# Attention on one core: a root chain for each tile of queries and keys, without rows in DRAM, and half of the wide high parts on GpSimd

## The chip, the cores and the metric

The kernel runs on one NeuronCore of one Trainium2 chip. The metric is the device time of one execution in microseconds. Engines are named as in the profile: PE is TensorE (PEld its weight loads), DVE VectorE, ACT ScalarE, POOL GpSimd, SP SyncE, whose queue here issues nearly all DMAs.

## The reference

A trunk of two layers over 1024 positions and 1024 features: a recurrent block with an MLP, then chunked band attention with an MLP. The stage that the change touches is the attention of the second layer:

```python
h = rmsnorm(x, kv_norm)
kv = (h @ w_kv).reshape(bsz, s, 2, N_HEADS, HEAD_DIM)
k = rmsnorm(kv[:, :, 0], k_norm)
v = kv[:, :, 1]
...
q = (rmsnorm(h, b_norm[j]) @ b_w_q[j]).reshape(bsz, s, N_HEADS, HEAD_DIM)
q = rmsnorm(q, b_q_norm[j])
...
sc = jnp.einsum('bhqd,bhkd->bhqk', qb, kb).astype(jnp.float32) * scale + bias
p = jax.nn.softmax(sc, axis=-1).astype(vb.dtype)
return jnp.einsum('bhqk,bhkd->bhqd', p, vb)
```

There are 16 heads of 64 features. Each query or key vector of 64 features is divided by the root of its mean square (rmsnorm with EPS 1e-6). A query sees its own chunk of 64 positions and the eight before it.

## The kernel before

Everything is held with features on partitions: a tile t (0 to 7) is 128 features, which is two heads, by 1024 positions, worked on in two halves h of 512. Products of 32-bit data are made of a high and a low part, three matmuls each (`mm`, L376 to L378).

In the attention stage the work of a tile is of two sorts.

*Projections* (`Proj`). For keys, queries and values in turn, 16 steps each (two halves by eight tiles of x, three matmuls a step) fill a bank `pj`. `normed` then normalizes a half of keys or queries: it scales it (q, L1726), squares it on ScalarE (L1729, L1732), and splits the squares in sh and sl (sl on GpSimd, L1735). Two matmuls (L1744, L1745) with a constant `band` sum the squares of each head. `band` is ones in 2 x 64 rows by 16 columns and is read at an offset, so that the four halves j of a tile (two of keys, two of queries) add their sums to different rows of one bank `nm`: 16 equal rows for each half and head. There is one `nm` bank, which is taken at j = 0. After j = 3 `roots` makes the inverse roots of all eight rows at once: Ln, Exp and Square on ScalarE (L1794, L1796, L1799), two operations on VectorE (L1801, which frees the bank, and L1805). One row of each 16 is written to DRAM (`rd`), and four DMAs read it back as `rb`, each spreading two rows of 512 numbers over 2 x 64 partitions. Then each half is multiplied by its rb on VectorE (L1752), split in 16-bit parts `ev` and `lo`, and moved by DMAs (`od`, `los`, ...) to where the heads need it.

*Units*. Each tile has eight: two heads e, two halves h, two pairs of query blocks u. For each of its two blocks qi of 128 queries a unit makes scores (PE s, L1963, L1964), adds the bias (L1967), takes Exp (L1974), and after the reciprocal of the sums (L1990, L1992) splits the weights in a high part on ScalarE (L1982) and a low part on VectorE (L1984). For h = 1 the blocks are 640 wide and their tiles are named t; for h = 0 they are narrower and named v. A DMA transpose turns each part (t<-t, v<-v, L1668), and matmuls with the values follow (po, L2010). `load_bias` fetches one bias per head and scales it on GpSimd (L1888).

The order of the instructions on each engine is written out when the kernel is built. A planner runs these chains with a cost for every operation (`c_act`, `c_dve`, `c_pool`, C_MOVE = 2.4 us for a move by DMA, C_ISSUE = 0.55 us to issue it); what becomes ready first stands first. A unit is begun when enough projection steps have been laid down (the first after START = 52, L38). On the chip each engine, SP's queue too, runs its list strictly in order: what stands behind a waiting instruction waits too.

Of the kernel before, what the change touches and what calls it, by code (L numbers as in the profile page):

```python
# [9 lines left out]
F32 = mybir.dt.float32  # L10
F32R = mybir.dt.float32r
F16 = mybir.dt.float16
AF = mybir.ActivationFunctionType
ALU = mybir.AluOpType

P = 128
T = 1024
D = 1024
NF = 8
# [46 lines left out]

def c_act(n):
    return 0.2 + n * 0.00082


def c_acts(n):
    return 0.28 + n * 0.000836


def c_dve(n):
    return 0.145 + n * 0.00105
# [105 lines left out]
def tile_yoco_rglru_chunk_attention(  # L182
# [43 lines left out]
    def gf(s="g"):  # L226
        return gp.tile([P, H2], F32, tag="g", name=nm(s))
# [28 lines left out]
    def wf():  # L256
        return wp.tile([P, H2], F32, tag="w", name=nm("wf"))
# [7 lines left out]
    def bank(tag=None):  # L265
        if tag is None:
            tag = ("pj", "tp", "sc", "pj", "tp", "sc", "po", "sc")[ring[0] % 8]
            ring[0] += 1
        if tag in BANKS:
            return ps1.tile([P, H2], F32, tag=tag, name=nm(tag), bufs=BANKS[tag])  # L270
        return loose.tile([P, H2], F32, tag=tag, name=nm(tag), bufs=(LOOSE if tag in LOOSE else WIDE)[tag])
# [23 lines left out]
    ones = onesr.bitcast(F32)  # L295
    eps = cp.tile([P, 1], F32, name="eps")
    pool.memset(eps, EPS)
    band = kp.tile([P, P + 96], F32R, name="band")
    pool.memset(band.bitcast(F32), 0.0)
    pool.memset(band.bitcast(F32)[0:64, 96:112], 1.0)  # L300
    pool.memset(band.bitcast(F32)[64:128, 112:128], 1.0)
    g_kv, g_q = vec[:, V_KVN, :], vec[:, V_BN, :]


# [1290 lines left out]
    x1d = dp.tile([NF, P, T], F32, name="x1d")  # L1595
    x2d = dp.tile([NF, P, T], F32, name="x2d")
    x3d = dp.tile([NF, P, T], F32, name="x3d")
    rd = dp.tile([NF, 8, H2], F32, name="rd")
    od = dp.tile([SPILL, 2, P, T], F32, name="od")
    hid = dp.tile([7, NQ, P, H2], F32, name="hid")  # L1600

# [60 lines left out]
    def move(dst, src):  # L1662
        dma(dst, src)
        return plan.use("sp", C_ISSUE) + C_MOVE
# [6 lines left out]
    class Proj:  # L1671


        def __init__(self, t):
            self.t = t
            self.Q = self.K = self.KL = None
            self.rb = [None] * 4
            self.split = [0, 0]
            self.added, self.spread = [Flag(plan) for _ in range(4)], [Flag(plan) for _ in range(4)]
            self.VS, self.V = [None, None], [None, None]  # L1680
            self.made = {(kind, h): Flag(plan) for kind in range(3) for h in range(2)}

# [39 lines left out]
        def normed(self, kind, h, ps):  # L1722
            keys = kind == KEYS
            yield scaled[h]
            q = gf("q")
            dve.scalar_tensor_tensor(q, ps, -1.0, R[h], ALU.mult, ALU.mult)  # L1726
            yield plan.use("dve", c_dve(H2))
            sh = wr("sh")
            act.activation(sh, q, AF.Square)  # L1729
            plan.use("act", c_act(H2))  # L1730
            s = wf()
            act.activation(s, q, AF.Square)  # L1732
            yield plan.use("act", c_act(H2))
            sl = wr("sl")
            SLE.tensor_tensor(sl, s, sh.bitcast(F32), ALU.subtract)  # L1735
            yield plan.use("pool", c_pool(2 * H2), True) if SLE is pool else plan.use("dve", c_dve(H2), True)
            j = 2 * kind + h
            if not j:
                yield nms
                self.ss = bank("nm")  # L1740
            else:
                yield self.added[j - 1]
            ones2 = band[:, 96 - 32 * j : 96 - 32 * j + P]
            pe.matmul(self.ss, lhsT=ones2, rhs=sh, start=j == 0, stop=False, skip_group_check=True)  # L1744
            pe.matmul(self.ss, lhsT=ones2, rhs=sl, start=False, stop=j == 3, skip_group_check=True)  # L1745
            yield plan.pe(2 * H2)
            self.added[j].set(plan.t)
            if j == 3:
                plan.start(self.roots())
            yield self.spread[j]  # L1750
            r = self.rb[j]
            dve.scalar_tensor_tensor(q, q, gk if keys else gq, r, ALU.mult, ALU.mult)  # L1752
            yield plan.use("dve", c_dve(H2), True)
            if keys:
                if not h:
                    self.K, self.KL = (gh("ev"), gh("od")), (gh("lo"), gh("los"))
                even, odd, low, lows = (x[:, hs(h)] for x in (*self.K, *self.KL))
            else:
                if not h:
                    self.Q, self.QL = (gh("ev"), gh("od")), gh("lo")  # L1760
                even, odd, low = (x[:, hs(h)] for x in (*self.Q, self.QL))
            act.activation(even, q, AF.Copy)
            ready = plan.use("act", c_act(H2))
            if not keys:
                act.activation(odd[OD], q[OD], AF.Copy)
                plan.use("act", c_act(H2))
            yield ready
            dve.tensor_tensor(low, q, even, ALU.subtract)
            yield plan.use("dve", c_dve(H2), True)
            self.split[kind] += 1  # L1770
            if self.split[kind] == 2:
                plan.start(self.moves(kind))

        def moves(self, kind):
# [13 lines left out]
            yield last  # L1788
            for h in range(2):
                self.made[kind, h].set(last)  # L1790

        def roots(self):
            ss, r = self.ss, gf("hr")
            act.activation(r, ss, AF.Ln, scale=1.0 / HD, bias=eps)  # L1794
            yield plan.use("act", c_act(H2))
            act.activation(r, r, AF.Exp, scale=-0.5)  # L1796
            yield plan.use("act", c_act(H2))
            x = wf()
            act.activation(x, r, AF.Square, scale=(0.5 / HD) ** 0.5)  # L1799
            yield plan.use("act", c_act(H2))  # L1800
            dve.scalar_tensor_tensor(x, ss, HD * EPS, x, ALU.add, ALU.mult)  # L1801
            last = plan.use("dve", c_dve(H2))
            nms.release(last)
            yield last
            dve.scalar_tensor_tensor(r, x, 1.5, r, ALU.subtract, ALU.mult)  # L1805
            yield plan.use("dve", c_dve(H2), True)
            move(rd[self.t], r[0:P:16])
            yield plan.busy["sp"] + C_MOVE
            for j in range(4):
                self.rb[j] = rb = gf("rb")  # L1810
                last = move(
                    rb,
                    rd[self.t, 2 * j : 2 * j + 2].unsqueeze(1).broadcast_to([2, HD, H2]),
                )
                self.spread[j].set(last)
            yield last

        def steps(self):
            for kind in (KEYS, QUERIES, VALUES):
# [73 lines left out]
    class Unit:  # L1893
# [54 lines left out]
        def score(self, qi):  # L1948
            e, i = self.e, self.i0 + qi
            pr, bias = projs[self.t], biases[2 * self.t + self.e]  # L1950
            h = i // 4
            k0 = max(0, i - 4) * P
            k1 = (i + 1) * P
            wdt = k1 - k0
            sc = sp.tile([P, 640], F32, tag="c", name=nm("sc"), bufs=NC) if h else gf("sc")
            qc = slice(i * P, (i + 1) * P)
            yield scs
            ps = double()
            for kh in range(2):
                a, b = max(k0, kh * H2), min(k1, (kh + 1) * H2)  # L1960
                if a >= b:
                    continue
                pe.matmul(ps[:, a:b], lhsT=pr.Q[e][:, qc], rhs=pr.K[e][:, a:b], start=True, stop=False)  # L1963
                pe.matmul(ps[:, a:b], lhsT=pr.Q[e][:, qc], rhs=pr.KL[e][:, a:b], start=False, stop=True)  # L1964
            yield plan.pe(2 * wdt)
            mx = tiny()
            dve.tensor_tensor_reduce(  # L1967
                sc[:, :wdt], ps[:, k0:k1], bias[:, 640 - wdt :],
                scale=c1, scalar=3e38, op0=ALU.add, op1=ALU.min, accum_out=mx,
            )  # L1970
            last = plan.use("dve", c_dve(wdt) + 0.08)
            scs.release(last)
            yield last
            act.activation(sc[:, :wdt], sc[:, :wdt], AF.Exp, scale=-1.0, bias=mx, accum_out=self.sums[:, qi : qi + 1])  # L1974
            self.summed[qi].set(plan.use("act", c_acts(wdt) + 0.19))
            yield self.rooted
            sm = self.sums[:, qi : qi + 1]
            if self.pieces is None:
                self.pieces = self.plane(), self.plane()
            off = qi * self.count[0] * P  # L1980
            hi, lo = (x[:, off : off + wdt] for x in self.pieces)
            act.activation(hi, sc[:, :wdt], AF.Copy, scale=sm)  # L1982
            yield plan.use("act", c_acts(wdt))
            dve.scalar_tensor_tensor(lo, sc[:, :wdt], sm, hi, ALU.mult, ALU.subtract)  # L1984
            self.scored[qi].set(plan.use("dve", c_dve(wdt) + 0.06, True))

# [395 lines left out]
```

## Time and profile before

| | us |
|---|---|
| runs shown: median of 2 (lowest, highest) | 2229.45 (2226.83, 2232.08) |
| the profiled execution | 2225.27 |
| its span | 2223.2 |
| PE busy in the span | 2027.9 |
| DVE, ACT, POOL busy in the span | 1490.2, 1104.1, 436.3 |

The span runs from the first to the last instruction of the program; the execution's own time has 2.1 us more. A row of a group view names the source line, the engine, the operation and its tiles as out<-in, then the count, the busy time, the mean time of one in ns and the idle time of the engine before it. A view of waits names the engine and operation that waited, then what ended the wait. A releaser is the one that came last by the profile; what made that one late has to be looked for one step further back.

### The profile page before, as it was taken

To read this page: it belongs to the slowest core of one execution; us is meant where nothing else is said; L and a number is where in the kernel's file an instruction comes from. 1 tells how busy PE (TensorE), PEld (TensorE's weight loads), DVE (VectorE), ACT (ScalarE), POOL (GpSimd) and SP (SyncE) were. 2 spreads that over 40 slices of the span, in tenths; PEclk is the share of its full clock that TensorE was granted. 3 is DMA by queue.
4 is the path that set the end of the run, shared out by engine and by line. 5 is a ranking of instruction groups with operands and counts; after the bars stand their busy time and mean duration, and the time that the engine had idled before them with its cause. 6 is when DMAs were issued, how large, how long until landed. Compare 5 with 4: busy or idle time off the path is not lost.

```text
span 2223.2 us, 27860 instructions
## 1 busy us (share of the span) xinstructions
PE 2027.9 (91%) x9209; PEld 1638.1 (74%) x9209; DVE 1490.2 (67%) x2340; ACT 1104.1 (50%) x1920; POOL 436.3 (20%) x429
## 2 busy tenths in 40 slices
PE   7999999999999999977687769539999999999999
PEld 6888888888888888855465546427888888888887
DVE  6898777666777766345655456357886667777743
ACT  6778454434345455435575457356553434444532
POOL 2000113222200001332443334311123223000000
PEclk9999999999999999988898889869999999999999
DMA  4012435444697835247777656868444444887833
GB/s 156 29 44 83 147 117 182 156 148 146 220 333 241 262 127 176 86 75 121 128 154 142 133 117 154 192 126 188 158 159 152 157 156 157 317 279 243 252 106 104
DMA packets 319297, 357.07 MB, mean 161 GB/s; under 512 B 163952, under 2 KB 166896, under 8 KB 319152
## 3 DMA queue, kind: packets, MB, share of 16 engines
q1 hardware_dynamic: 319008, 355.24, 56.0%
q8 instruction: 72, 1.18, 0.2%
q14 instruction: 73, 0.60, 0.1%
q10 hardware_dynamic: 144, 0.05, 0.0%
HBM read 230.28 MB, written 80.87 MB: 140 GB/s over the span
## 4 chain that ended last, share of the span: by engine, by line
PE 79%; DMA 11%; DVE 3%; SPq 2%; issue 2%; ACT 2%; POOL 2%; DVEq 0%; POOLq 0%; ACTq 0%
PE pj L376 11%; PE pj L377 11%; PE pj L378 11%; PE tp L377 5%; PE tp L378 5%; PE tp L376 5%; DMA rb<-rd 5%; PE p L377 4%; PE sc L376 4%; PE sc L377 4%; PE p L378 4%; PE sc L378 4%; PE p L376 4%; PE po L2010 2%; DMA t<-t 1%
## 5 line engine op out<-in xcount | busy, mean ns | idle before, releaser
L376 PE MATMUL pj<-h,wh 128*128 128x512 f32 x1260 | 511.8, 406 | 7.3 <-ACT h L2032 7.2
L377 PE MATMUL pj<-l,wh 128*128 128x512 f32 x1260 | 497.6, 395 | 0.8 <-DVE l L2034 0.8
L378 PE MATMUL pj<-h,wl 128*128 128x512 f32 x1260 | 497.4, 395 | 0.0
L1140 ACT ACTIVATE wh<-raw 128x512 fp32r<-128x512 f32 x333 | 205.6, 624 | 168.7 <-PE pj L377 43.5
L376 PEld LDWEIGHTS pj<-h,wh 128*128 128x128 f32 x1260 | 242.0, 192 | 59.5 <-ACT h L2032 8.0
L1141 DVE TENSOR_TENSOR wl<-raw,wh 128x512 fp32r<-128x512 f32 x333 | 254.0, 770 | 39.3 <-ACT wh L1140 36.2
L378 PEld LDWEIGHTS pj<-h,wl 128*128 128x128 f32 x1260 | 240.7, 191 | 52.0
L377 PEld LDWEIGHTS pj<-l,wh 128*128 128x128 f32 x1260 | 241.7, 192 | 49.4 <-DVE l L2034 1.5
L389 ACT ACTIVATE h<-raw 128x512 fp32r<-128x512 f32 x224 | 139.3, 628 | 217.5 <-PE sc L377 61.8
L378 PE MATMUL tp<-h,wl 128*128 128x512 f32 x554 | 215.7, 389 | 1.5 <-DVE wl L342 1.5
L377 PE MATMUL tp<-l,wh 128*128 128x512 f32 x554 | 215.8, 389 | 0.3 <-DVE l L390 0.3
L376 PE MATMUL tp<-h,wh 128*128 128x512 f32 x554 | 215.6, 389 | 0.0
L390 DVE TENSOR_TENSOR l<-raw,h 128x512 fp32r<-128x512 f32 x224 | 153.5, 692 | 76.1 <-ACT h L389 73.1
L1415 ACT ACTIVATE s<-s 128x512 f32<-128x512 f32 x125 | 79.0, 633 | 203.7 <-DVE s L1414 195.0
L2010 PEld LDWEIGHTS <-vs 128*128 128x128 f16 x576 | 53.5, 103 | 157.4 <-issue 131.0
L377 PE MATMUL p<-l,wh 128*128 128x512 f32 x384 | 150.7, 392 | 9.3 <-DVE l L672 9.3
L376 PE MATMUL sc<-h,wh 128*128 128x512 f32 x394 | 153.3, 389 | 0.0
L378 PE MATMUL sc<-h,wl 128*128 128x512 f32 x394 | 153.3, 389 | 0.0
L377 PE MATMUL sc<-l,wh 128*128 128x512 f32 x394 | 153.3, 389 | 0.0
L376 PE MATMUL p<-h,wh 128*128 128x512 f32 x384 | 151.1, 393 | 1.0 <-ACT wh L555 1.0
L378 PE MATMUL p<-h,wl 128*128 128x512 f32 x384 | 150.3, 391 | 0.0
L1149 POOL TENSOR_TENSOR raw<-raw,raw 128x512 f32<-128x512 f32 x29 | 49.9, 1721 | 372.1 <-DVE wl L1141 274.0
(323 smaller groups left out, 3599.2 us busy)
## 6 DMA issues: line engine op xcount, KB each, us to landing
raw<-hid SPq DMA_DIRECT2D x224, 256.0 KB
hid<-s SPq DMA_DIRECT2D x221, 256.0 KB
raw<-in_w_down SPq DMA_DIRECT2D x192, 256.0 KB
raw<-in_w_up SPq DMA_DIRECT2D x128, 256.0 KB
s<-in_w_down SPq DMA_DIRECT2D x64, 256.0 KB
raw<-in_w_kv SPq DMA_DIRECT2D x32, 256.0 KB
rb<-rd SPq DMA_DIRECT2D x32, 256.0 KB
raw<-in_w_in SPq DMA_DIRECT2D x30, 256.0 KB
```

The costliest lines, as they stand in the source:

```text
L376: pe.matmul(ps, lhsT=wh, rhs=xh, start=start, stop=False, skip_group_check=more)
L377: pe.matmul(ps, lhsT=wh, rhs=xl, start=False, stop=False, skip_group_check=more)
L378: pe.matmul(ps, lhsT=wl, rhs=xh, start=False, stop=stop, skip_group_check=more)
L389: act.activation(h, src, AF.Copy)
L390: dve.tensor_tensor(l, src, h.bitcast(F32), ALU.subtract)
L1140: act.activation(wh, raw, AF.Copy)
L1141: dve.tensor_tensor(wl, raw, wh.bitcast(F32), ALU.subtract)
L1149: pool.tensor_tensor(raw[A11], raw[A11], raw[A21], ALU.add)
L1415: act.activation(out, out, AF.Square)
L2010: pe.matmul(dst, lhsT=st, rhs=src, start=start, stop=final, skip_group_check=self.u == 1)
```

## The change

Each half of keys or queries gets its own chain. The constant `band` becomes `bdiag`, ones in two blocks of 64 x 64: the two matmuls now leave each head's sum on all 64 of its partitions. So the root, made in `normed` itself with the same five operations, already stands where it is used, and the row in DRAM and its four spreads go. The chain runs four times per tile where `roots` ran once, and each run takes the one `nm` bank and frees it.

In `score`, the high part of the weights moves from ScalarE to GpSimd where h and qi are both 1: 32 of the 64 high parts that are 640 wide. The planner gets a cost for it, `c_phi`. START is 52 before and after.

```diff
+def c_phi(n):
+    return 0.08 + n * 0.001
...
-    band = kp.tile([P, P + 96], F32R, name="band")
-    pool.memset(band.bitcast(F32), 0.0)
-    pool.memset(band.bitcast(F32)[0:64, 96:112], 1.0)
-    pool.memset(band.bitcast(F32)[64:128, 112:128], 1.0)
+    bdiag = kp.tile([P, P], F32R, name="bdiag")
+    pool.memset(bdiag.bitcast(F32), 0.0)
+    pool.memset(bdiag.bitcast(F32)[0:64, 0:64], 1.0)
+    pool.memset(bdiag.bitcast(F32)[64:128, 64:128], 1.0)
...
-            j = 2 * kind + h
-            if not j:
-                yield nms
-                self.ss = bank("nm")
-            else:
-                yield self.added[j - 1]
-            ones2 = band[:, 96 - 32 * j : 96 - 32 * j + P]
-            pe.matmul(self.ss, lhsT=ones2, rhs=sh, start=j == 0, stop=False, skip_group_check=True)
-            pe.matmul(self.ss, lhsT=ones2, rhs=sl, start=False, stop=j == 3, skip_group_check=True)
+            yield nms
+            ss = bank("nm")
+            pe.matmul(ss, lhsT=bdiag, rhs=sh, start=True, stop=False)
+            pe.matmul(ss, lhsT=bdiag, rhs=sl, start=False, stop=True)
             yield plan.pe(2 * H2)
-            self.added[j].set(plan.t)
-            if j == 3:
-                plan.start(self.roots())
-            yield self.spread[j]
-            r = self.rb[j]
+            r = gf("hr")
+            act.activation(r, ss, AF.Ln, scale=1.0 / HD, bias=eps)
...
+            act.activation(r, r, AF.Exp, scale=-0.5)
...
+            x = wf()
+            act.activation(x, r, AF.Square, scale=(0.5 / HD) ** 0.5)
...
+            dve.scalar_tensor_tensor(x, ss, HD * EPS, x, ALU.add, ALU.mult)
+            last = plan.use("dve", c_dve(H2))
+            nms.release(last)
+            yield last
+            dve.scalar_tensor_tensor(r, x, 1.5, r, ALU.subtract, ALU.mult)
+            yield plan.use("dve", c_dve(H2), True)
             dve.scalar_tensor_tensor(q, q, gk if keys else gq, r, ALU.mult, ALU.mult)
...
-        def roots(self):
...
-            move(rd[self.t], r[0:P:16])
-            yield plan.busy["sp"] + C_MOVE
-            for j in range(4):
-                self.rb[j] = rb = gf("rb")
-                last = move(
-                    rb,
-                    rd[self.t, 2 * j : 2 * j + 2].unsqueeze(1).broadcast_to([2, HD, H2]),
-                )
-                self.spread[j].set(last)
...
-            act.activation(hi, sc[:, :wdt], AF.Copy, scale=sm)
-            yield plan.use("act", c_acts(wdt))
+            if h and qi:
+                pool.tensor_scalar(hi, sc[:, :wdt], sm, 1.0, ALU.mult, ALU.mult)
+                yield plan.use("pool", c_phi(wdt), True)
+            else:
+                act.activation(hi, sc[:, :wdt], AF.Copy, scale=sm)
+                yield plan.use("act", c_acts(wdt))
```

Since the planner lays the whole stage out anew, instructions move on every engine. Two places show how. On SP's queue before, in the third tile (t = 2), the row is written, and the four spreads stand between two pairs of wide transposes (a number behind a name tells one buffer from another):

```order
L286 DMA od<-l_9373 128x512
L286 DMA rd<-hr_9319 8x512
L1668 DMA_TRANSPOSE t_9500<-t_9407 128x10x128
L1668 DMA_TRANSPOSE t_9502<-t_9408 128x10x128
L286 DMA rb_9514<-rd 128x1x512
L286 DMA rb_9516<-rd 128x1x512
L286 DMA rb_9518<-rd 128x1x512
L286 DMA rb_9520<-rd 128x1x512
L1668 DMA_TRANSPOSE t_9549<-t_9460 128x10x128
L1668 DMA_TRANSPOSE t_9551<-t_9461 128x10x128
```

The same stretch of SP's queue in the changed kernel, from the bias of the same place on:

```order
L290 DMA s_9469<-in_relb 128x640
L290 DMA od<-h_9431 128x512
L290 DMA od<-l_9432 128x512
L290 DMA od_9342<-ev_9341 64x1024 x2
L290 DMA los_9344<-lo_9343 64x1024 x2
L290 DMA ev_9341<-ev_9341 64x1024
L290 DMA lo_9343<-lo_9343 64x1024
L290 DMA raw_9515<-in_w_q 128x512
L290 DMA raw_9517<-in_w_q 128x512
L1671 DMA_TRANSPOSE t_9530<-t_9447 128x10x128
L1671 DMA_TRANSPOSE t_9532<-t_9448 128x10x128
```

The write and the spreads are gone, and the moves of the tile's keys (od, los, ev, lo) now stand ahead of these transposes. In all SP's list is 40 DMAs shorter.

On PE before, in the first tile (t = 0), where the second and third pair of sums go into the one bank nm_8232, among the projection's matmuls:

```order
L1744 MATMUL nm_8232<-sh_8245,band 128x512
L1745 MATMUL nm_8232<-sl_8263,band 128x512
L376 MATMUL pj_8239<-h_7318,wh_8134 128x512
L377 MATMUL pj_8239<-l_7319,wh_8134 128x512
L378 MATMUL pj_8239<-h_7318,wl_8145 128x512
L1744 MATMUL nm_8232<-sh_8252,band 128x512
L1745 MATMUL nm_8232<-sl_8271,band 128x512
```

The second pair on PE in the changed kernel, in the same tile:

```order
L380 MATMUL pj_8289<-h_6090,wh_8201 128x512
L381 MATMUL pj_8289<-l_6091,wh_8201 128x512
L382 MATMUL pj_8289<-h_6090,wl_8210 128x512
L1740 MATMUL nm_8297<-sh_8246,bdiag 128x512
L1741 MATMUL nm_8297<-sl_8268,bdiag 128x512
L380 MATMUL pj_8289<-h_6098,wh_8201 128x512
L381 MATMUL pj_8289<-l_6099,wh_8201 128x512
```

Each pair now has a buffer nm of its own number in the same bank, so it stands behind the read of the pair before it. In the first tile 30, 33 and 21 projection matmuls stand between its four pairs.

More of the change, by code (lines that the diff above doesn't have):

```diff
@@ L1597, in tile_yoco_rglru_chunk_attention @@
     x3d = dp.tile([NF, P, T], F32, name="x3d")
-    rd = dp.tile([NF, 8, H2], F32, name="rd")
     od = dp.tile([SPILL, 2, P, T], F32, name="od")
@@ L1676, in __init__ @@
             self.Q = self.K = self.KL = None
-            self.rb = [None] * 4
             self.split = [0, 0]
-            self.added, self.spread = [Flag(plan) for _ in range(4)], [Flag(plan) for _ in range(4)]
             self.VS, self.V = [None, None], [None, None]
@@ L1736, in normed @@
             yield plan.use("pool", c_pool(2 * H2), True) if SLE is pool else plan.use("dve", c_dve(H2), True)
-            j = 2 * kind + h
-            if not j:
-                yield nms
-                self.ss = bank("nm")
-            else:
-                yield self.added[j - 1]
-            ones2 = band[:, 96 - 32 * j : 96 - 32 * j + P]
-            pe.matmul(self.ss, lhsT=ones2, rhs=sh, start=j == 0, stop=False, skip_group_check=True)
-            pe.matmul(self.ss, lhsT=ones2, rhs=sl, start=False, stop=j == 3, skip_group_check=True)
-            yield plan.pe(2 * H2)
-            self.added[j].set(plan.t)
-            if j == 3:
-                plan.start(self.roots())
-            yield self.spread[j]
-            r = self.rb[j]
+            yield nms
+            ss = bank("nm")
+            pe.matmul(ss, lhsT=bdiag, rhs=sh, start=True, stop=False)
+            pe.matmul(ss, lhsT=bdiag, rhs=sl, start=False, stop=True)
+            yield plan.pe(2 * H2)
+            r = gf("hr")
+            act.activation(r, ss, AF.Ln, scale=1.0 / HD, bias=eps)
+            yield plan.use("act", c_act(H2))
+            act.activation(r, r, AF.Exp, scale=-0.5)
+            yield plan.use("act", c_act(H2))
+            x = wf()
+            act.activation(x, r, AF.Square, scale=(0.5 / HD) ** 0.5)
+            yield plan.use("act", c_act(H2))
+            dve.scalar_tensor_tensor(x, ss, HD * EPS, x, ALU.add, ALU.mult)
[4 more added lines that the diff above has]
+            yield plan.use("dve", c_dve(H2), True)
             dve.scalar_tensor_tensor(q, q, gk if keys else gq, r, ALU.mult, ALU.mult)
@@ L1790, in moves @@
                 self.made[kind, h].set(last)
-        def roots(self):
[L1793 to L1806, printed above, removed]
-            move(rd[self.t], r[0:P:16])
-            yield plan.busy["sp"] + C_MOVE
-            for j in range(4):
-                self.rb[j] = rb = gf("rb")
-                last = move(
-                    rb,
-                    rd[self.t, 2 * j : 2 * j + 2].unsqueeze(1).broadcast_to([2, HD, H2]),
-                )
-                self.spread[j].set(last)
-            yield last
         def steps(self):
```

## The prediction, made before the change was run

> **What bounds the kernel now.** First the page: which engine is full, and where it is not. The columns of the second part are 40 slices of 55.6 us each.
>
> ```profile
> span 2223.2 us, 27860 instructions
> PE 2027.9 (91%) x9209; PEld 1638.1 (74%) x9209; DVE 1490.2 (67%) x2340; ACT 1104.1 (50%) x1920; POOL 436.3 (20%) x429
> PE   7999999999999999977687769539999999999999
> PEclk9999999999999999988898889869999999999999
> ```
>
> TensorE is the bound nearly everywhere; it falls to 3 to 8 tenths in nine of the slices 18 to 27, the attention stage, and its clock falls there too. Only there is idle time worth much. Then the sums by stretch: the stage before its first long wait, with the waits, and its tail.
>
> ```profile
> core 0: us, PE busy (x) PEld busy (x) DVE busy (x) ACT busy (x) POOL busy (x), PEclk, DMA share, GB/s
> 962.00:1483.00 521.00, 357.92 (x1824) 266.44 (x1823) 276.83 (x562) 280.07 (x583) 189.59 (x216) 0.85 0.71 136
> 915.00:962.00 47.00, 47.00 (x208) 38.66 (x206) 16.03 (x25) 21.41 (x39) 21.71 (x20) 1.00 0.17 57
> 1483.00:1560.00 77.00, 62.33 (x330) 45.69 (x330) 53.43 (x107) 46.10 (x89) 8.76 (x18) 0.85 0.84 194
> ```
>
> Of 521 us TensorE is idle for 163. Its timeline shows that this is not spread: one wait of 12 to 20 us for each of the eight tiles t. Asked as eight stretches (first, last and sum), then the seven stretches between them (sum):
>
> ```profile
> 962.37:978.69 16.32, 0.00 (x1) 0.00 (x0) 5.83 (x8) 4.29 (x7) 3.02 (x4) 0.63 1.01 126
> ...
> 1463.05:1483.54 20.49, 0.00 (x1) 0.00 (x0) 5.12 (x8) 5.23 (x10) 0.00 (x0) 0.63 0.62 70
> sum 129.70, PE 0.02 PEld 0.01 DVE 34.13 ACT 27.80 POOL 5.94; mean PE 0.00 PEld 0.00 DVE 4.27 ACT 3.47 POOL 0.74
> ...
> sum 391.47, PE 357.52 PEld 266.43 DVE 243.24 ACT 252.27 POOL 183.64; mean PE 51.07 PEld 38.06 DVE 34.75 ACT 36.04 POOL 26.23
> ```
>
> In the eight waits nothing computes: 129.7 us with TensorE at zero, VectorE at 26%. Between them TensorE is 91% busy. What ends the waits, by the waits between 962 and 1484 us (total, times, longest):
>
> ```profile
> DVE q L1752 <- DMA rb<-rd: 118.2, 31, 4.8
> PE po L2010 <- DMA t<-t: 73.4, 10, 20.5
> PE po L2010 <- DMA v<-v: 38.7, 7, 18.7
> PE nm L1745 <- POOL sl L1735: 28.6, 6, 16.3
> PE po L2010 <- DVE o L2023: 13.4, 3, 12.0
> ```
>
> TensorE's rows name transposes, GpSimd and VectorE, none of them rb. The timelines of SP, VectorE and TensorE around the third wait say why all the same:
>
> ```profile
> 1080.75 3.18 SPq L1668 DMA_TRANSPOSE t<-t  x2
> 1084.02 9.23 SPq L286 DMA_DIRECT2D rb<-rd  x4
> 1093.36 14.69 SPq L1668 DMA_TRANSPOSE t<-t  x2
> 1091.76 0.75 DVE L1752 SCALAR_TENSOR_TENSOR q<-q,gk,rb 128x512 f32<-128x512 f32 x1 [1.34 <-DMA rb<-rd]
> 1097.11 0.75 DVE L1752 SCALAR_TENSOR_TENSOR q<-q,gk,rb 128x512 f32<-128x512 f32 x1 [3.93 <-DMA rb<-rd]
> 1108.97 0.37 PE L2010 MATMUL po<-t,vs 128*128 128x256 f16 x1 [16.04 <-DMA t<-t]
> ```
>
> The four spreads take SP 9.2 us to issue, and the two transposes behind them 14.7 us where two earlier ones took 3.2. VectorE gets one rb every 5.35 us (1091.76 to 1097.11), and stands still for 3.9 of them. Of the DMA view between 1088 and 1096 us, where they run alone:
>
> ```profile
> DMA  1111111111111111111111111111111111111111
> q1 hardware_dynamic: 194, 0.39, 13.0%
> ```
>
> 13% of 16 engines is two engines. At one rb in 5.35 us the four spreads need 21 us in this way, once per tile, whatever else waits in the queue.
>
> **The change, part by part.** (1) The row write, the four spreads and the waits for them go: minus 8 writes and 32 spreads on SP, and minus the eight waits. Would the transposes then be in time? In the third wait they would be issued at 1084.0, would be out of SP 3.2 us later, and TensorE reaches them at 1092.9 (1108.97 less 16.04): 5.7 us are left for the landing, which after the late issue (1093.36 + 14.69 = 1108.05) took 0.9. So the whole wait goes, there and, I assume, in the other seven: **minus 129.7**.
>
> (2) The clock. What TensorE does after such a wait, and after a short one:
>
> ```profile
> 979.29 0.63 PE L376 MATMUL pj<-h,wh 128*128 128x512 f32 x1
> ...
> 983.13 0.63 PE L376 MATMUL pj<-h,wh 128*128 128x512 f32 x1
> ...
> 984.54 0.39 PE L378 MATMUL pj<-h,wl 128*128 128x512 f32 x1
> 984.77 0.39 PE L376 MATMUL pj<-h,wh 128*128 128x512 f32 x1
> 1129.26 0.50 PE L1745 MATMUL nm<-sl,band 128*128 128x512 f32 x1 [2.75 <-POOL sl L1735]
> 1130.50:1133.80 3.30, 3.30 (x11) 2.57 (x9) 1.02 (x5) 2.03 (x6) 3.30 (x4) 0.50 0.97 181
> ```
>
> From 979.29 to 983.13 nine matmuls start 0.43 us apart, later 0.23: some 2.1 us are lost after each long wait, eight times: **minus 17**. The Trainium skill's page "TensorE: Matmul & The Clock Gate" ("HAM oscillation") says that an idle window of about 3.4 us halves the clock until such a window has been busy; by its figure this term is an estimated 8 x 1.7 = 14, and new waits shorter than 3.4 us would leave the clock alone. The trace only half agrees: a wait of 2.75 us was followed by 3.3 us at a clock of 0.50. So a new wait of that size costs itself and 1.65 us more.
>
> (3) Three more root chains per tile, 24 in all, and 32 high parts moved from ScalarE to GpSimd (h and qi both 1: always 640 wide). The rows:
>
> ```profile
> L1794 ACT ACTIVATE hr<-nm,eps x8: 667/671/690, 943.8 to 1443.7; 128x512 f32<-128x512 f32 x8
> L1796 ACT ACTIVATE hr<-hr x8: 616/618/632, 944.5 to 1447.4; 128x512 f32<-128x512 f32 x8
> L1799 ACT ACTIVATE wf<-hr x8: 612/618/622, 946.5 to 1450.8; 128x512 f32<-128x512 f32 x8
> L1801 DVE SCALAR_TENSOR_TENSOR wf<-nm,wf x8: 668/680/692, 947.2 to 1451.7; 128x512 f32<-128x512 f32 x8
> L1805 DVE SCALAR_TENSOR_TENSOR hr<-wf,hr x8: 659/692/1523, 948.0 to 1453.1; 128x512 f32<-128x512 f32 x8
> L1982 ACT ACTIVATE t<-sc,t x64: 811/815/830, 1003.7 to 1535.8; 128x640 f16<-128x640 f32 x64
> L1984 DVE SCALAR_TENSOR_TENSOR t<-sc,t,t x64: 859/879/1975, 1004.6 to 1537.4; 128x640 f16<-128x640 f32 x64
> L1888 POOL TENSOR_SCALAR s<-s,heads x16: 799/858/1824, 919.2 to 1492.7; 128x640 f32<-128x640 f32 x16
> L1744 PE MATMUL nm<-sh,band x32: 387/402/628, 932.1 to 1433.2; 128*128 128x512 f32 x32
> ```
>
> ScalarE: 24 x (0.67 + 0.62 + 0.62) = 45.8, less 32 x 0.815 = 26.1: plus 19.7. VectorE: 24 x (0.68 + 0.69) = 32.9. GpSimd: no row shows this operation with a 16-bit output; the nearest is the bias scaling of the same size, 0.80 to 1.82, median 0.86: 32 x 0.86 = 27.5, at most 58. TensorE: the same count, against another constant: nothing. All of it can hide: to the 391 us between the waits come what was done inside them and what is new, which makes VectorE 243 + 34 + 33 = 310 (79%), ScalarE 252 + 28 + 20 = 300 (77%), GpSimd 184 + 6 + 28 = 218 (56%). But these queues run in order, now at 62%, 64% and 47%, and even so TensorE idles for 34 us between the waits. So the term lies between 0 (all hidden) and 33 + 20 + 28 = 81 (nothing hidden; 111 with GpSimd at 58). I take **plus 30**, near the lower end, because the idle share of each queue stays above a fifth, and because the chain gets shorter for the units: a key half is scaled when its own sum is done, not after four halves.
>
> The page "GPSIMD Engine Reference" of the Trainium skill ("1. Specifications") speaks against moving the high parts: GpSimd shares its SBUF interfaces with VectorE and contends with VectorE instructions that have two SBUF inputs. The row of L1984, such an instruction, runs from 0.86 to 1.98 with a median of 0.88, so some of that is seen. If each moved operation met one of them at the worst price, VectorE would gain another 32 x 1.1 = 35 us, its share would be 88%, and with the same third of it landing the sum would be 12 higher.
>
> (4) The constant is set by as many memsets before the stage: nothing. START is 52 in both files.
>
> **Sum.** The profiled execution took 2225.3 (span 2223.2 and 2.1 around it): 2225.3 - 129.7 - 17 + 30 = 2108.6. The two runs have a median 4.2 above it; I give 2110.
>
> **Rivals.** *B, the side engines take over the bound.* Nearly all of (3) lands on TensorE's path, through VectorE at 79 to 88%: 2225.3 - 146.7 + 81 = 2160, and 2190 with GpSimd at its dearest row. For it: rows of L1984 and L1888 that take twice their median, so that the planner's fixed costs are missed. Against it: the 38% of VectorE's time between the waits that is idle now. *C, the one nm bank, slower than before.* Each chain now holds the only bank from its first matmul until VectorE has read it: 0.40 + 0.40 + 0.67 + 0.62 + 0.62 + 0.68 = 3.4 us, 32 times, and TensorE stands in order before the next pair; behind it wait the projections and every unit. If it waits one whole hold at each pair, with 1.65 for the clock, that is 32 x 5.05 = 162: 2270. It eats the gain of 117 from 2.0 us of waiting at each pair. Against it: in the new order 21 to 33 matmuls stand between the first tile's pairs, 4.8 to 7.6 us at 0.23 each, more than a hold. *D, the change does not remove the cause.* If transposes and moves are slow by themselves, the waits shrink only by part: with half of 147 back and 30 to pay, 2182, and with a third 2206. Against it: the 3.2 us of the undisturbed pair. *E, better:* (3) is hidden entirely, and GpSimd's lag behind the spreads goes too (28.6 less the 16.3 already counted): 2225.3 - 146.7 - 12.3 = 2066.
>
> **Numbers.** Forecast, 2078 to 2139: 0.68. B: 0.14, of which 0.02 is at its dear end over 2185. E, below 2078: 0.10. D: 0.05, about the 2% line. C: 0.03. The range 2070 to 2162 reaches into E and B and leaves out the rest of them, D and C, together less than 0.2. This kernel's measurement tells some 2% from no change, 44.6 us: faster means below 2184.9. Faster 0.90 (forecast, E and most of B), same 0.07, slower 0.03.
>
> **What would show it.** Right: no rb row on VectorE; SP's pairs of wide transposes near 3.2 us; no TensorE idle stretch over 10 us between 962 us and the stage's end; the stage's clock above 0.93; the stage some 115 us shorter and the rest unchanged to a few us. B shows as VectorE above 85% with waits of TensorE for t<-t or s spread evenly; C as TensorE waiting at nm for VectorE's read; D as waits of over 8 us for transposes that SP issued in time. I am wrong if a fixed cost per tile comes back under another name.

## The result, and the profile after

The changed kernel takes 2083.05 us (median of two runs, 2082.7 to 2083.39) against 2229.45: a ratio of 0.9343 (95% interval 0.9296 to 0.9391), 146 us or 6.6% faster. A second comparison, with four runs of the changed kernel, gave 0.9362 (0.9346 to 0.9378).

First the page of the changed kernel, the same rows as were shown of the kernel before:

```profile
span 2081.6 us, 27921 instructions
PE 2013.9 (97%) x9209; PEld 1629.0 (78%) x9209; DVE 1546.2 (74%) x2388; ACT 1118.8 (54%) x1960; POOL 479.8 (23%) x461
PE   8999999999999999999989898799999999999999
PEclk9999999999999999999999999899999999999999
```

The hole in TensorE's row is nearly closed. The span is 141.6 us shorter. The stretches of the attention stage of the changed kernel, cut so that the middle one is 141.6 us shorter than its counterpart before:

```profile
core 0: us, PE busy (x) PEld busy (x) DVE busy (x) ACT busy (x) POOL busy (x), PEclk, DMA share, GB/s
962.00:1341.40 379.40, 336.95 (x1790) 252.80 (x1789) 315.49 (x587) 287.02 (x606) 221.44 (x234) 0.96 0.72 162
915.00:962.00 47.00, 47.00 (x209) 38.93 (x208) 27.43 (x38) 28.32 (x51) 26.08 (x24) 1.00 0.30 81
1341.40:1418.40 77.00, 68.05 (x366) 49.03 (x366) 56.54 (x118) 45.65 (x93) 16.54 (x29) 0.87 0.90 186
```

TensorE's idle time in the three stretches was 645.0 - 467.2 = 177.8 us; now it is 503.4 - 452.0 = 51.4. That is 126 us of the 142. The other 15 are the same matmuls done in less busy time (467.2 - 452.0): the clock, whose mean over the middle stretch went from 0.85 to 0.96. TensorE's own waits in that stretch of the changed kernel (total, times, longest), and the longest of them in its timeline:

```profile
PE po L1993 <- DVE o L2006: 15.4, 5, 8.6
PE nm L1741 <- POOL sl L1736: 7.6, 2, 5.8
PE s L1942 <- DVE t L1946: 6.1, 6, 3.8
PE nm L1740 <- DVE wf L1751: 3.9, 5, 1.9
PE po L1993 <- DMA v<-v: 2.7, 4, 1.0
PE po L1993 <- DMA t<-t: 0.8, 2, 0.5
1176.32 2.29 PE L1993 MATMUL po<-t,vs 128*128 128x256 f16 x12 [8.60 <-DVE o L2006]
```

Before, 112 us of waits for transposes (73.4 and 38.7) stood here; now 3.5. What is left names VectorE first, but no wait is longer than 8.6 us. On SP's queue of the changed kernel the two pairs of wide transposes that follow take what the undisturbed pair took before (3.2 us), and not 14.7. Not every pair does, but of all 64 single transposes the dearest takes 3.4 us, where it took 10.8 (last two rows: min, median and max in ns, the kernel before and then the changed one):

```profile
1074.95 3.13 SPq L1671 DMA_TRANSPOSE t<-t  x2
...
1079.53 2.93 SPq L1671 DMA_TRANSPOSE t<-t  x2
...
L1668 SPq DMA_TRANSPOSE t<-t x64: 1259/1484/10807, 1005.3 to 1541.6; - x64
L1671 SPq DMA_TRANSPOSE t<-t x64: 1252/1384/3374, 995.6 to 1398.0; - x64
```

### The profile page after: what moved, and what is told of

Its sections match the earlier page's. It is cut to its first block, busy times and chain, and to the rows that moved or that the text cites. A ratio compares the mean times of both kernels' runs of the same rounds, so it can differ in the third digit from the quotient of the medians.

```text
span 2081.6 us, 27921 instructions
## 1 busy us (share of the span) xinstructions
PE 2013.9 (97%) x9209; PEld 1629.0 (78%) x9209; DVE 1546.2 (74%) x2388; ACT 1118.8 (54%) x1960; POOL 479.8 (23%) x461
## 4 chain that ended last, share of the span: by engine, by line
PE 80%; DMA 6%; DVE 6%; issue 3%; POOL 2%; ACT 1%; SPq 1%; DVEq 0%; POOLq 0%
PE pj L380 11%; PE pj L381 11%; PE pj L382 11%; PE tp L381 5%; PE tp L382 5%; PE tp L380 5%; PE p L381 4%; PE sc L381 4%; PE p L382 4%; PE p L380 4%; PE sc L382 4%; PE sc L380 4%; DMA raw<-in_w_down 2%; PE po L1993 1%; DMA t<-t 1%
## 5 line engine op out<-in xcount | busy, mean ns | idle before, releaser
L380 PE MATMUL pj<-h,wh 128*128 128x512 f32 x1260 | 502.9, 399 | 0.2 <-DVE s L1466 0.2
L382 PE MATMUL pj<-h,wl 128*128 128x512 f32 x1260 | 492.0, 390 | 0.0
L381 PE MATMUL pj<-l,wh 128*128 128x512 f32 x1260 | 491.5, 390 | 0.0
L380 PEld LDWEIGHTS pj<-h,wh 128*128 128x128 f32 x1260 | 237.5, 188 | 50.4 <-DVE s L1466 1.1
L340 POOL TENSOR_TENSOR raw<-raw,vec 128x512 f32<-128x512 f32 x48 | 55.4, 1155 | 313.9 <-DMA raw<-in_w_kv 288.2
```

The source lines that it names most:

```text
L340: pool.tensor_tensor(raw, raw, gains, ALU.mult)
L380: pe.matmul(ps, lhsT=wh, rhs=xh, start=start, stop=False, skip_group_check=more)
L381: pe.matmul(ps, lhsT=wh, rhs=xl, start=False, stop=False, skip_group_check=more)
L382: pe.matmul(ps, lhsT=wl, rhs=xh, start=False, stop=stop, skip_group_check=more)
```

## The experiments

Times are medians; a ratio is to the kernel before on the same chip, with its 95% interval.

### Are the spreads alone to blame?

The kernel before, in its own order, without write and spreads:

```diff
-            r = self.rb[j]
+            r = self.hr
...
-            move(rd[self.t], r[0:P:16])
+            plan.use("sp", C_ISSUE)
...
-                self.rb[j] = rb = gf("rb")
-                last = move(rb, rd[self.t, 2 * j : 2 * j + 2].unsqueeze(1).broadcast_to([2, HD, H2]))
+                last = plan.use("sp", C_ISSUE) + C_MOVE
```

> The kernel before, in its own order, without the row write and the four spreads; VectorE multiplies by the rows that stand in the bank's image (hr) instead, so keys and queries are scaled by wrong rows. No chain is added and no high part moved. Theory S (the eight long waits come from the spreads alone, by way of SP's queue and of VectorE's wait): 2225 - 147 = 2078, that is 2070 to 2090, and the difference to the changed kernel's 2083 is what its added chains and moved high parts really cost. Rival O (the new order pays, the spreads are only part): above 2110, with waits of TensorE over 8 us left.

Measured: 2071.96 us, ratio 0.9311 (0.9297 to 0.9325). Theory S holds, rival O falls: the old order with nothing added gains all of it. Its waits of TensorE over 962 to 1341 us:

```profile
PE nm L1744 <- POOL sl L1734: 16.0, 7, 3.8
PE po L2006 <- DVE o L2019: 11.9, 5, 7.9
PE po L2006 <- DMA t<-t: 1.8, 2, 1.2
```

It is also the price list of the change: 0.9362 - 0.9311 = 0.0051 of 2227 us, 11 us (some 7 to 16 by the two intervals), is what the added chains, the moved high parts and their new order cost.

### Why are the spreads slow?

Each spread as two DMAs of one row to 64 partitions, and nothing else changed:

```diff
-                last = move(
-                    rb,
-                    rd[self.t, 2 * j : 2 * j + 2].unsqueeze(1).broadcast_to([2, HD, H2]),
-                )
+                for a in range(2):
+                    dma(rb[a * HD : (a + 1) * HD], rd[self.t, 2 * j + a : 2 * j + a + 1].broadcast_to([HD, H2]))
+                last = plan.use("sp", C_ISSUE) + C_MOVE
```

> The kernel before, each spread issued as two DMAs that take one row to 64 partitions, so that the slowest running dimension is 64 and not 2. Same data, same order. Theory S2 (the spreads are slow because two DMA engines of 16 carry them): the four spreads land in some 3 to 5 us instead of 21, DMA share near them far above 13%, no TensorE wait over 10 us, time 2085 to 2110. Rival R (the round trip through DRAM and its place in the queue is slow whatever the shape): SP's transposes behind stay late, 2150 to 2225.

Measured: 2105.49 us, ratio 0.9465 (0.9449 to 0.948). Theory S2 holds: nearly four fifths of what the kernel without rows gained (0.0535 of 0.0689) come back although every byte still makes its way through DRAM. SP's timeline of this kernel around the fourth tile, the DMA queue and its issues between 1107 and 1115 us (count, KB each, median us to landing), VectorE's waits for rb in the whole stage, and TensorE's for transposes up to 1440 us:

```profile
1109.25 5.18 SPq L286 DMA_DIRECT2D rb<-rd  x8
1114.53 3.22 SPq L1668 DMA_TRANSPOSE t<-t  x2
...
q1 hardware_dynamic: 3188, 1.61, 94.2%
...
rb<-rd SPq DMA_DIRECT2D x8, 128.0 KB, 3.2
...
DVE q L1752 <- DMA rb<-rd: 1.6, 4, 0.4
...
PE po L2009 <- DMA t<-t: 19.6, 18, 4.5
PE po L2009 <- DMA v<-v: 12.7, 11, 4.1
```

Half a spread lands 3.2 us after its issue, the engines' share is 94% (in a stretch that also holds packets of transposes) where it was 13%, and the transposes behind take their 3.2 us again. This is what the Trainium skill's page "DMA: Bandwidth & Descriptors" states under "Why a DMA increments its semaphore by 16 and not by 1": the slowest running dimension on each side of a transfer sets how many of the 16 engines carry it. With a 2 on one side it is two engines, with 64 and 64 sixteen; the trace agrees with the first by the 13%, and with the second by the share near full. Of what is missing to the kernel without rows (34 us), TensorE's short waits for transposes, 32 us in all and none over 4.5, are the likely part; no run tests it.

### Which way does it reach TensorE?

Write and spreads as before, but VectorE reads hr instead (the first hunk of the first diff alone):

> The kernel before with its write and its spreads, in its own order, but VectorE does not read what they bring (it multiplies by hr, wrong rows). SP's queue is as before, VectorE's wait is gone. If SP's queue is the main route (transposes behind the spreads): the eight waits of TensorE stay at 10 us or more, 2170 to 2225. If VectorE's wait for rb is the main route: under 2130. I expect the first, since the transposes behind the third tile's spreads were out of SP only 0.9 us before TensorE went on.

Measured: 2229.28 us, ratio 1.0006 (0.9995 to 1.0017). Nothing. VectorE's 118 us of waits for rb, the first of the rows of waits in the prediction, were by themselves worth nothing. TensorE's waits between 962 and 1486 us in this kernel, and its SP row behind the third spreads:

```profile
PE po L2011 <- DMA t<-t: 76.5, 13, 19.8
PE po L2011 <- DMA v<-v: 51.4, 7, 17.9
PE nm L1745 <- POOL sl L1735: 26.2, 6, 15.9
...
1094.18 14.61 SPq L1668 DMA_TRANSPOSE t<-t  x2
```

With VectorE free, the unit's transposes are as late as ever (14.61 us, 14.69 before). So the late transposes are enough for the whole loss. What VectorE's waits would cost with the transposes in time stays open, for no run has these waits alone. The next run asks the same of the order: the planner is told the truth about the spreads.

```diff
+            base = plan.busy["sp"]
             for j in range(4):
...
-                last = move(
+                move(
...
+                last = base + 2.4 + 5.35 * (j + 1)
                 self.spread[j].set(last)
```

> The kernel before, with the planner told when a spread really lands: 5.35 us after the one before it, not 0.55. The work is the same, only the order moves. Theory S: VectorE no longer stands for rb (under 40 us of such waits, 119.5 before), but the transposes that stand behind the spreads on SP are still late: 2150 to 2215. Rival P (the planner's wrong cost is the whole loss): 2080 to 2120.

Measured: 2223.52 us, ratio 0.9992 (0.9981 to 1.0002). VectorE's waits for rb fall to 5 us, as theory S said; the time does not move, and lies outside the 2150 to 2215 that it gave.

```profile
DVE q L1752 <- DMA rb<-rd: 4.9, 4, 2.5
PE po L2012 <- DMA v<-v: 92.7, 11, 22.1
PE po L2012 <- DMA t<-t: 39.8, 15, 15.8
```

TensorE waits 132.5 us for transposes. So this order, with VectorE's waits gone, is worth nothing as long as the transposes stand behind the spreads. The last run of this group takes them out of SP's queue:

```diff
-                last = move(
-                    rb,
-                    rd[self.t, 2 * j : 2 * j + 2].unsqueeze(1).broadcast_to([2, HD, H2]),
-                )
+                act.dma_start(rb, rd[self.t, 2 * j : 2 * j + 2].unsqueeze(1).broadcast_to([2, HD, H2]))
+                last = plan.use("sp", C_ISSUE) + C_MOVE
```

> The kernel before with its four spreads issued from ScalarE's queue at the place that the plan had for them, everything else as it was. The spreads still run on two DMA engines and still take 21 us. Theory Q (what hurts is that the transposes stand behind the spreads in one queue): the waits of TensorE for t<-t and v<-v fall below 5 us each; the issue may now hold up ScalarE for some 9 us per tile, so 2110 to 2170. Rival E (the two DMA engines themselves are the jam, since every transpose needs all sixteen): the long waits stay, 2190 to 2230.

Measured: 2214.53 us, ratio 0.9952 (0.9933 to 0.9971). Neither theory's picture is whole. Timelines of ScalarE and SP around the third tile, and waits of TensorE and VectorE between 962 and 1486 us:

```profile
1081.50 11.09 ACTq L1811 DMA_DIRECT2D rb<-rd  x4
1092.64 0.80 ACT L1980 ACTIVATE v<-sc,t 128x128 f16<-128x128 f32 x2 [10.96 <-issue]
...
1080.49 12.33 SPq L1668 DMA_TRANSPOSE t<-t  x3
...
PE po L2008 <- DMA t<-t: 45.8, 15, 7.7
PE po L2008 <- DVE o L2021: 35.2, 7, 18.1
PE po L2008 <- DMA v<-v: 11.1, 5, 3.5
DVE q L1752 <- DMA rb<-rd: 83.2, 19, 5.6
```

The waits for transposes fall from 112 to 57 us and none is longer than 7.7, so standing behind the spreads in one queue is part of it. But three transposes beside the spreads still take 12.3 us to issue. ScalarE now spends 8 to 14 us of each tile on issuing (11.1 in this one), and VectorE still waits 83.2 us for rb; either can be what makes VectorE's o late (35.2). How much of the remaining loss is the two engines that the transposes share with the spreads, how much ScalarE and how much VectorE's waits, this run does not tell apart.

### What the rest costs

The moved high parts back on ScalarE, at the same places of the order:

```diff
             if h and qi:
-                pool.tensor_scalar(hi, sc[:, :wdt], sm, 1.0, ALU.mult, ALU.mult)
+                act.activation(hi, sc[:, :wdt], AF.Copy, scale=sm)
                 yield plan.use("pool", c_phi(wdt), True)
```

> The changed kernel as it is, beside the next three on one chip. 2083, ratio 0.932 to 0.937. With the kernel without rows at a ratio of 0.9311 this gives what the added chains and the moved high parts cost together: theory S says 5 to 13 us, where the prediction had 30.

> The changed kernel in its own order, its 32 moved high parts back on ScalarE at the place planned for GpSimd. ScalarE gets 26 us more, GpSimd some 30 less. Theory H (idle shares hide both): within 6 us of the changed kernel. Rival G (GpSimd's work slows VectorE's two-input operations, and that lands): VectorE's busy time falls by 15 us or more and the time by over 8. Rival A (ScalarE is the tighter queue): slower by over 8.

Measured: 2085.17 us, ratio 0.9362 (0.9346 to 0.9378) for the changed kernel, 2086.72 us, 0.9373 (0.9359 to 0.9387) with the high parts back. The intervals overlap: moving half of the wide high parts made no difference that can be measured, although VectorE's busy time falls from 1543.6 to 1533.4 us with the move undone. (A plan that itself keeps them on ScalarE was not run.) All wide high parts on GpSimd:

```diff
-            if h and qi:
+            if h:
```

> The changed kernel with all 64 high parts of 640 on GpSimd instead of 32, and the planner told so. GpSimd gets some 30 us more (about 60% of the stage), ScalarE 26 less. Theory H: within 10 us of the changed kernel, likelier above. Rival G: VectorE's busy time rises by another 10 to 20 us, and the time by 10 to 30.

Measured: 2104.61 us, ratio 0.9448 (0.9434 to 0.9462): 19 us slower than with half. VectorE's busy time is 1559.0 us, 15 more, so rival G's numbers come out, for the second half of the moves. That this is the way it costs time is not shown: the order is new, and GpSimd itself has 34 us more to do (515.6 against 481.6). Then VectorE's load, unplanned, planned, and planned behind the chain:

```diff
-            dve.scalar_tensor_tensor(r, x, 1.5, r, ALU.subtract, ALU.mult)
+            r2 = gf("hs")
+            for _ in range(3):
+                dve.scalar_tensor_tensor(r2, x, 1.5, r, ALU.subtract, ALU.mult)
```

> The changed kernel with the last operation of each of its 32 root chains done three times on VectorE (into a tile of its own), unplanned: 64 x 0.69 = 44 us more, VectorE then at some 86% of the stage. Theory H (what is hidden is hidden because VectorE has a fifth of its time idle): part lands, 5 to 20 us. Rival B (VectorE is already what TensorE waits for): 30 to 44 us. If nothing lands (under 3), VectorE is not near the bound at all.

> As the kernel with the tripled last operation on VectorE, but the planner is told of the 64 operations. The unplanned load cost 35 of its 44 us. Theory V (VectorE is now what TensorE waits for): the order cannot help, 25 to 44 us over the changed kernel, 2110 to 2130. Rival T (it cost that much only because the order did not know of it): within 12 us, 2083 to 2097.

> The same 64 operations on VectorE, told to the planner, but behind the scaling of the half and read by nobody: VectorE has as much to do, and no chain gets longer. If VectorE's share of time decides (theory V): like the run before it, 2105 to 2130. If the length of the chain decides: within 10 us of the changed kernel, 2083 to 2095.

Measured: 2119.78 us, ratio 0.952 (0.9506 to 0.9534); 2113.27 us, 0.9495 (0.9475 to 0.9514); 2109.8 us, 0.9477 (0.9459 to 0.9495). Against 0.9362 that is 35, 30 and 26 us for 44 us of nominal work; VectorE's busy time, 1543.6 us in the changed kernel beside them, grew by 52, 65 and 64. Theory H's 20 us is passed even where no chain is longer and the planner knows. The stage (915 to 1425 us) of the last of the three and of the changed kernel in its second profile:

```profile
915.00:1425.00 510.00, 445.17 (x2270) 332.44 (x2269) 447.57 (x784) 355.64 (x735) 282.58 (x285) 0.94 0.67 148
```

```profile
915.00:1425.00 510.00, 458.76 (x2388) 346.69 (x2387) 403.68 (x746) 364.33 (x756) 266.06 (x287) 0.95 0.71 160
```

VectorE goes from 79% to 88% of the stretch, and TensorE falls behind. The counterpart is a kernel in which VectorE has less to do:

```diff
-            yield scaled[h]
             q = gf("q")
-            dve.scalar_tensor_tensor(q, ps, -1.0, R[h], ALU.mult, ALU.mult)
-            yield plan.use("dve", c_dve(H2))
+            act.activation(q, ps, AF.Copy)
+            yield plan.use("act", c_act(H2))
```

> The changed kernel, where a half of keys or queries leaves its bank by a copy on ScalarE instead of a product with R on VectorE. The factor R of the row norm cancels in the norm per head, but for EPS, which is then added to squares without it: that small part of the computation is changed. VectorE has 32 x 0.69 = 22 us less, ScalarE 20 us more, and no half waits for R. Theory V: 5 to 20 us faster than the changed kernel, 2063 to 2078. If ScalarE is the tighter engine: the same or slower.

Measured: 2089.13 us, ratio 0.939 (0.937 to 0.941): no gain, if anything a small loss. So VectorE is not simply the bound of the changed kernel: 44 us of nominal work more cost over half of themselves (0.4 to 0.7 of the busy time that they became), 22 us less bring nothing while ScalarE gets 20 more. Whether ScalarE takes back what VectorE gives, or the chance of another order does, stays open.

## Why the prediction was right

*The verdict.* 2083 lies in the range (2070 to 2162) and at the low end of the forecast case (2078 to 2139), 27 us below the 2110 named. By the ratios of the runs, some 19 of the 27 are the third term, and 7 the first two together. The stage became 141.6 us shorter, where the prediction named some 115.

*(1) The eight waits, minus 129.7: right.* No wait over 10 us is left, and TensorE's idle time fell by 126. The step that carried it, SP's queue with the pair of transposes that would be in time without the spreads, is what the runs confirm. It was worked out for the third wait alone and assumed for the other seven; the kernel without rows bears that out. VectorE's waits for rb, which the prediction showed first, carried nothing by themselves: taking VectorE's dependence away changed nothing, nor did telling the planner.

*(2) The clock, minus 17: right,* 141.6 - 126.4 = 15.2 in the two profiles, and 17.8 us less busy time of TensorE in the kernel without rows (2010.1 against 2027.9). *(4), nothing: nothing seen against it.*

*(3) The added chains and high parts, plus 30: mis-sized.* Measured 11. It was taken between 0 and 81 from the idle shares of the queues, with no row that could price it. The bound was sound and the counts were right, but the durations were not: the page's busy time of VectorE rose by 56 us where 33 were forecast, of GpSimd by 43.5 for 28, of ScalarE by 14.7 for 19.7. So more busy time was added than thought and less of it landed. Of the 56, the moved high parts account for some 10 (1543.6 less 1533.4, with the move undone), and they cost no time that can be measured: undoing the move gained nothing. What VectorE loses beside GpSimd's other operations (below) was not priced by a run.

*The rivals.* B did not come, though it is near: VectorE is at 83% of the long stretch (315.5 of 379.4 us) where 85% was named as the sign, and the next 44 us of nominal work on it land by more than half. C did not: TensorE's waits at nm for VectorE's read are 3.9 us in five times in the long stretch, 0.8 on average. D did not. E was half right: the kernel without rows shows that the waits and the clock alone are worth 153.5 us (0.0689 of 2227), 7 more than the 146.7 of the sum; but it was not GpSimd's lag at nm, which is still 16.0 us there.

## What to carry to other kernels

Read a long wait one step further back than its row: here 118 us of VectorE's waits for rb were by themselves worth nothing, and what counted was who stood behind the same transfers in the DMA queue. Look at the slowest running dimension of every broadcast by DMA: here a 2 went with 13% of the engines and held up all that stood behind it, and a 64 in its place gave back most of the loss with two lines. An idle share says that added work can hide, not how much of it will: the first 56 us of VectorE's busy time cost 11 together with everything else, the next 52 to 65 cost 26 to 35.

## What the runs showed of the hardware

*A transfer on two DMA engines can hold up what stands behind it while the others idle.* Between 1088 and 1096 us the spreads of the kernel before used 13% of the engines, which is two of sixteen, and yet transposes behind them took 14.7 us instead of 3.2. All that time, from 1093.4 to 1107.6 us, the share stays at one tenth but for one short burst (40 slices):

```profile
DMA  1111111111119991111111111111111111111111
```

Another issuing queue did not free them (12.3 us for three), and kept ScalarE, which issued the spreads there, for 11.1 us in the third tile.

*GpSimd beside VectorE.* The multiplication of a half by its root reads two tiles in SBUF. It took 0.75 us in the rows of before that the prediction shows; in the changed kernel its minimum is 724 ns, but for keys its median is 1120. After that row, the timelines of VectorE and GpSimd show what runs beside one of the long ones:

```profile
L1757 DVE SCALAR_TENSOR_TENSOR q<-q,gk,hr x16: 724/1120/1785, 940.1 to 1318.3; 128x512 f32<-128x512 f32 x16
...
940.06 1.67 DVE L1757 SCALAR_TENSOR_TENSOR q<-q,gk,hr 128x512 f32<-128x512 f32 x1
...
939.39 1.78 POOL L346 TENSOR_TENSOR wl<-raw,wh 128x512 fp32r<-128x512 f32 x1 [0.74 <-ACT wh L343]
941.14 1.74 POOL L1736 TENSOR_TENSOR sl<-wf,sh 128x512 fp32r<-128x512 f32 x1
```

In the kernel before, GpSimd's own operation with two inputs had these times:

```profile
L1735 POOL TENSOR_TENSOR sl<-wf,sh x32: 1262/1286/1879, 925.7 to 1428.1; 128x512 fp32r<-128x512 f32 x32
```

Here two such take 1.78 and 1.74 us, and VectorE's operation more than twice its minimum: both lose. Before, 31 of VectorE's 32 multiplications ran while GpSimd did nothing and took 0.75 us; the one of 1.54 us, at 1307.0, ran beside GpSimd's wl of 1.28 us:

```profile
L1752 DVE SCALAR_TENSOR_TENSOR q<-q,gk,rb x16: 750/752/1544, 958.1 to 1471.7; 128x512 f32<-128x512 f32 x16
L1752 DVE SCALAR_TENSOR_TENSOR q<-q,gq,rb x16: 750/752/753, 969.0 to 1482.4; 128x512 f32<-128x512 f32 x16
```

That the Trainium skill's page "GPSIMD Engine Reference" ("1. Specifications") names such contention was said ahead; the runs add its size, up to some 1 us on an operation of 0.72.

*A scaled copy of 640 numbers a partition to 16 bits on GpSimd,* which no row showed before, costs at its median what it cost on ScalarE (0.80 us against 0.815), with a long tail (min, median, max in ns):

```profile
L1962 POOL TENSOR_SCALAR t<-sc,t x32: 797/802/2492, 983.7 to 1392.0; 128x640 f16<-128x640 f32 x32
```
